# Normalised, transposed and split token halves: made once and kept in DRAM, or made again for the late round

## The chip, the cores and the metric

One core of a Trainium2 chip runs the whole kernel. The metric is the device time of one execution in microseconds (us), the median of several runs. TensorE (PE) does matmuls and transposes and writes PSUM; VectorE (DVE), ScalarE (ACT) and GpSimd (POOL) do elementwise work; SyncE (SP) issues every DMA of this kernel from one queue, in order. A DMA that has to wait for a semaphore holds all DMAs behind it in that queue.

## The reference

Two sequences (1024 tokens, 1024 channels each) go through two layers:

```
(shift, scale, gate) = silu(c) @ W_ada + b_ada
h = RMSNorm(x) * (1 + scale) + shift
P = h @ W_in                          # all inputs of four mixers
x = x + gate * RMSNorm(concat(A, B, C, D) @ W_out)
```

A is latent attention, B RWKV-7, C Mamba-2, D gated DeltaNet, the last three in both directions; each is gated with a slice z of P.

## The kernel before, in words

A unit is a pair (sequence s, layer l); units 0 to 3 are (0,0), (1,0), (0,1), (1,1). A unit has an in-projection (32 tiles of 128 columns of W_in, for each of two halves of 512 tokens), four mixers and an out-projection. The mixers run in two streams: D, then A on the right side of the on-chip memory, C, then B on the left; a mixer takes the place of the one before it on its side. Every tile of P goes to DRAM and is loaded by the mixer that needs it.

The in-projection of the next unit and the out-projection of the unit before run beside the mixers. Their matmuls are one "bulk" stream on line 458 (`paced`), in groups of five, each group released by a tiny memset on POOL (line 462). The in-projection comes in two rounds. The early round gives the tiles of D and the xbc tiles of C for both halves; the late round gives the other 19 tiles, beginning with zc0 and zc1 (the gate of C) and later wa and rkv (for B), cq (for A). The late round begins with the half that the early round ended with, since this half is still there, and then needs the first half again:

```
early = (0, W_D + W_B), (1, W_D + W_B)
late = (1, W_REST), (0, W_REST)
...
run_in(0, (0, W_D), (1, W_D + W_B))
ahead(MIX * EA // 100, 45, lambda: run_in(0, (0, W_B + W_REST), (1, W_REST)))
```

Unit 0 has the second order, with one change of half more. So of 13 makings of a half, five make a half a second time: (0,0) and (0,1) of unit 0 and the half 0 of units 1, 2 and 3, here called (1,0), (2,0), (3,0) by unit and half.

A half is made by `norm_in`, in two groups of 256 tokens: x is loaded (two DMAs of 512 KB), squared and summed on ACT, scaled on DVE by the root (line 289), transposed in 128x128 blocks on TensorE (line 294), and for each block row written twice by ACT (lines 296 and 298: once in full, once rounded to hh); DVE subtracts the two to give hl (line 299). hh and hl together carry h at nearly full precision, each [128, 8, 512]. Each of these two buffers exists once, so a new half can be written only when the last matmul on the old half has read it. An in-projection tile is 8 x 3 matmuls: wh with hh, wh with hl, wl with hh, where wh and wl are the like parts of the weights, made from w by ACT and DVE (lines 327 and 329) just in time.

The order of the instructions on each engine, the DMA queue among them, is laid down at build time by a planner: it runs a model of the engines over the program and takes, of what is ready in the model, what has the best priority. `ahead` and `behind` spread the priorities of the bulk over those of the mixers.

Of the kernel before, what the change touches and what calls it, by code (L numbers as in the profile page):

```python
# [21 lines left out]
D = 1024  # L22
# [86 lines left out]
class Body:  # L109
    def __init__(self, ctx, tc, A, outs, sl=None):  # L110
        self.tc, self.nc, self.A, self.outs = tc, tc.nc, A, outs
        self.n = 0
        self.side = "left"
        self.span = None
        nc = tc.nc
        self.cp = ctx.enter_context(tc.tile_pool(name="cp", bufs=1))
        self.dr = ctx.enter_context(tc.tile_pool(name="dr", bufs=1, space=DRAM))
        self.banks = 3
        self.held = None
        self.token = self.t(self.cp, [1, 1], tag="token")  # L120
        self.gate, self.run = None, 0
        self.ident = self.const(self.cp, "ident")
        self.blk = self.const(self.cp, "blk")
        self.bsel = self.const(self.cp, "bsel")
        self.cc = self.t(self.cp, [128, 4], tag="cc")
        nc.vector.memset(self.cc[:, 0:1], -0.5)
        nc.vector.memset(self.cc[:, 1:2], EPS)
        nc.vector.memset(self.cc[:, 2:3], 0.5)
        nc.vector.memset(self.cc[:, 3:4], 1.0)
        self.mhalf, self.eps, self.phalf, self.one1 = (self.cc[:, i:i + 1] for i in range(4))  # L130

    def open_io(self, ctx):
        """the pools of the projections"""
        self.pj = self.pool(ctx, "pj")
        self.sp = self.pool(ctx, "sp", 2)
        self.pps = self.pool(ctx, "pps", 2, PSUM)
# [20 lines left out]
    def sumsq(self, ps, col, sq, n, rhs, w, start=True, stop=True):  # L157
        """ps[:, col:col+w] = per-token sums over the channels of sq[:, 128 n : 128 n + 128]"""
        for x in range(2):
            self.nc.tensor.matmul(ps[64 * x:64 * x + 64, col:col + w], sq[:, n * 128 + 64 * x:n * 128 + 64 * x + 64], rhs,  # L160
                                  start=start, stop=stop)
# [98 lines left out]

    def stage_in(self, s, L, l, xsrc, Pd, parts=((0, W_ORDER), (1, W_ORDER))):
        """parts: (token half, tiles); the half of the part before is still there"""
        for hf, names in parts:
            if self.held is None or self.held[0] != (Pd, hf):
                self.spread()
                hh = self.t(self.pj, [128, 8, 512], F32R, tag="hh")
                hl = self.t(self.pj, [128, 8, 512], F32R, tag="hl")
                self.norm_in(s, L, xsrc, hf, hh, hl)
                self.held = (Pd, hf), hh, hl
            for name in names:  # L270
                self.spread()
                self.in_tile(l, name, hf, *self.held[1:], Pd)
# [59 lines left out]
    def out_tiles(self, l, ch, hh, hl, kqs, at=lambda kq: kq):  # L332
        """products of 4 token tiles with a quarter of the columns of w_out, over the quarters kqs of its rows"""
        nc, pj = self.nc, self.pj
        pss = [self.t(self.pps, [128, 2, 256], tag="pj") for _ in range(2)]
        for n, kq in enumerate(kqs):
            w = self.t(pj, [128, 2, 256], tag="w", bufs=2)
            self.dma(w, self.A["w_out"][l, ch, kq // 2][:, (kq % 2) * 512:(kq % 2) * 512 + 512].rearrange("p (k c) -> p k c", k=2))
            with self.urgent():
                wh, wl = self.split_w(w, [128, 2, 256])  # L340
            for i in range(4):
                ps = pss[i // 2][:, i % 2]
                c = slice(i * 128, (i + 1) * 128)
                for k in range(2):
                    a, b = hh[:, at(kq) * 2 + k, c], hl[:, at(kq) * 2 + k, c]
                    first, last = n == 0 and k == 0 and i % 2 == 0, n == len(kqs) - 1 and k == 1
                    for m, (u, w2) in enumerate(((a, wh), (a, wl), (b, wh))):
                        self.paced(TO, ps, u, w2[:, k], dict(start=first and m == 0, stop=last and m == 2, skip_group_check=True))
        return pss
# [50 lines left out]
    def stage_out_last(self, s, L, l, xsrc, od, dst, parts, ctx=None):  # L400
        """the last output in parts (token half, quarters of the rows of w_out, whether the sums begin or end),
        while the mixers of the later quarters still run"""
        nc, v, pj, sp = self.nc, self.nc.vector, self.pj, self.sp
# [52 lines left out]
    def paced(self, n, *mm):  # L456
        """a matmul of a bulk stream: groups of n, each issued after the group before has begun"""
        m = self.nc.tensor.matmul(*mm[:3], **mm[3]).ins  # L458
# [9 lines left out]

# [1 line left out]
    def urgent(self):  # L470
# [8 lines left out]
    def behind(self, p0, p1, n, fs):  # L479
        """emit fs with priorities spread over those from p0 to p1"""  # L480
        keep = self.tc.cur_priority
# [33 lines left out]
    def invert(self, pool, r, d, src):  # L515
        """r = inverses of the unit triangular 32 x 32 diagonal blocks of src, transposed"""
        nc = self.nc
# [14 lines left out]
    def merge(self, pool, psp, r, d, src, dst):  # L532
        """dst = inverse of the unit triangular 64 x 64 blocks of src from the inverses r of their diagonal blocks"""
        nc = self.nc
# [32 lines left out]
    def pair_t(self, psp, dst, src, scale=None):  # L567
        """dst[(c parity, t), (c // 2, x, e)] = transposes of 8 chunks of both heads of src, times scale[(c parity, t), c // 2, x]"""
        ps = self.bank(psp)
# [8 lines left out]
    def dma_pair(self, dst, src, swap):  # L578
        """dst[(x or 1 - x, t), c, e] (DRAM) = src[(c parity, t), (c // 2, x, e)]"""
        sv = src.rearrange("p (j x e) -> p j x e", j=4, x=2)  # L580
# [5 lines left out]
    def head_sum(self, ps, sq, n):  # L586
        """ps[half, i] = sums over the channels of the head of the other half"""
        for i in range(n):
# [3 lines left out]
    def heads_back(self, psp, y):  # L592
        """transposes back to channels: y[(1 - x, t), c, pr, e] -> [(pr, e), x, c, t]"""
        ps = self.t(psp, [128, 512], tag="w")
# [4 lines left out]
    def rows2(self, t, r0, q):  # L599
        """rows r0 to r0 + 256 and quarter q of the tokens"""  # L600
        return t[r0:r0 + 256, q * 256:q * 256 + 256].rearrange("(r p) t -> p r t", r=2)
# [43 lines left out]

# [1 line left out]
    def mixer_b(self, L, Pd, l, od):  # L647
# [8 lines left out]
    def rwkv_norm(self, p, psp, L, Pd, q, y, yd, bon, od, free):  # L656
        """normalisation, bonus and gate of a quarter of the tokens"""
        nc, v = self.nc, self.nc.vector
# [292 lines left out]

# [1 line left out]
    def mixer_d(self, L, Pd, l, od):  # L953
# [120 lines left out]
    def gdn_norm(self, p, psp, L, Pd, q, y, yd, fq, od, free):  # L1074
        """normalisation and gate of a quarter of the tokens"""
        nc, v = self.nc, self.nc.vector
# [163 lines left out]

# [1 line left out]
    def mixer_c(self, L, Pd, l, od):  # L1242
# [149 lines left out]

# [1 line left out]
    def mixer_a(self, L, Pd, l, od):  # L1394
# [103 lines left out]
    def attend(self, p, psp, qd, kd, krd, VO, ot):  # L1498
        """softmax of every head; the maxima of a head are found during the head before"""
        nc, v = self.nc, self.nc.vector  # L1500
# [73 lines left out]
    def mixers(self, L, Pd, l, od, which="dcab"):  # L1574
        """the streams right (d, a) and left (b, c)"""
        p = dict.fromkeys(("left", "right"), self.tc.cur_priority)
# [8 lines left out]
    def last_mixers(self, L, Pd, l, od, io):  # L1585
        """three streams: d, c on the right; b; a in the place of the projections"""
        p0 = self.tc.cur_priority
# [15 lines left out]
    def full(self):  # L1603
# [11 lines left out]
        def run_in(u, *parts):  # L1615
            s, l = units[u]
            if u not in P:
                P[u] = self.t(self.dr, [NWT * 128, 1024], tag="P", bufs=2)
            self.stage_in(s, L[l], l, src(s, l), P[u], parts)

# [15 lines left out]
        def ahead(w, n, f):  # L1636
            """emit f with priorities spread over the next w, n steps"""
            p = self.tc.cur_priority
# [4 lines left out]
        def out_last(parts, ctx=None):  # L1643
            s, l = units[3]
            self.stage_out_last(s, L[l], l, src(s, l), o[3], self.outs[s], parts, ctx)

        early = (0, W_D + W_B), (1, W_D + W_B)
        late = (1, W_REST), (0, W_REST)
# [76 lines left out]
```

## Time and profile before

| | |
|---|---|
| median of 3 runs | 4894.8 us (4888.07 to 4915.18) |
| span of the profiled execution | 4894.9 us |
| TensorE busy | 4389.3 us, 90% |
| VectorE busy | 3343.1 us, 68% |
| ScalarE busy | 2178.9 us, 45% |
| mean granted clock of TensorE | 0.878 of full speed |
| DMA | 671.79 MB, 137 GB/s in the mean |

The profiled execution's own time is its span; nothing that was timed lies around it. Busy time of TensorE counts a matmul from its start to a modelled end, so it is more than the time in which it takes columns. Shares are means over the whole span; what a half costs has to be read where it is made.

### The profile page before, as it was taken

How to read it: one execution, taken by the hardware profiler on the slowest of the kernel's cores; microseconds unless marked ns; L12 is line 12 of the kernel's file. 1: busy time of each engine (PE TensorE's matmuls, PEld its weight loads, DVE VectorE, ACT ScalarE, POOL GpSimd, SP SyncE). 2: the span in 40 equal slices, each digit the busy share in tenths (PEclk: the TensorE clock that was granted, in tenths of full speed). 3: DMA queues.
4: the chain of work that ended last, by engine and by line, in shares of the span. 5: the costliest groups of instructions: out<-in, count | busy, mean ns of one | idle time of the engine just before them, and what ended most of it. 6: DMA issues, size and time to landing. Idle time of an engine off the chain costs nothing.

```text
span 4894.9 us, 100724 instructions
## 1 busy us (share of the span) xinstructions
PE 4389.3 (90%) x38644; PEld 3358.2 (69%) x38644; DVE 3343.1 (68%) x6837; ACT 2178.9 (45%) x4734; POOL 397.6 (8%) x2093
## 2 busy tenths in 40 slices
PE   6879798999997988999989898899989989898997
PEld 3667576766776776756767667776767766776686
DVE  2488877566578787566459778657546968856666
ACT  2444363563434534443454453455344354344333
POOL 0101010000101000000011100000011100000001
PEclk8889898998997987989989798798889979878788
DMA  4444264242453546363345353545145535455224
GB/s 144 136 148 138 99 192 132 87 131 99 135 171 126 160 127 192 109 197 110 112 154 162 109 174 117 174 139 147 63 133 165 163 111 158 130 181 156 85 86 137
DMA packets 495063, 671.79 MB, mean 137 GB/s; under 512 B 149752, under 2 KB 265976, under 8 KB 493560
## 3 DMA queue, kind: packets, MB, share of 16 engines
q1 hardware_dynamic: 494584, 665.36, 43.6%
q8 instruction: 306, 5.01, 0.4%
q14 instruction: 173, 1.42, 0.1%
HBM read 486.53 MB, written 178.57 MB: 136 GB/s over the span
## 4 chain that ended last, share of the span: by engine, by line
PE 49%; DVE 13%; DMA 10%; issue 3%; ACT 3%; SPq 1%; POOL 0%; DVEq 0%; POOLq 0%; ACTq 0%
PE pj L458 21%; PE b L824 3%; PE b L1568 2%; PE b L551 2%; DVE iA L522 1%; PE b L558 1%; SPq L144 1%; PE b L1456 1%; PE b L1555 1%; PE pj L243 1%; PE w L863 1%; DVE wl L329 1%; DVE GT L537 1%; PE b L1524 1%; PE y L1220 1%
## 5 line engine op out<-in xcount | busy, mean ns | idle before, releaser
L458 PE MATMUL pj<-hh,wl 128*128 128x512 f32 (+1 forms) x2048 | 848.2, 415 | 32.0 <-DVE wl L329 18.4
L458 PE MATMUL pj<-hh,wh 128*128 128x512 f32 (+1 forms) x2048 | 854.6, 418 | 11.9 <-DVE iT L529 3.2
L458 PE MATMUL pj<-hl,wh 128*128 128x512 f32 (+1 forms) x2048 | 849.7, 415 | 16.9 <-POOL token L462 16.6
L327 ACT CAST wh<-w 128x512 fp32r<-128x512 f32 x640 | 395.1, 618 | 775.4 <-PE pj L458 495.1
L329 DVE TENSOR_TENSOR wl<-w,wh 128x512 fp32r<-128x512 f32 x640 | 446.6, 699 | 245.3 <-ACT wh L327 211.8
L458 PEld LDWEIGHTS pj<-hh,wl 128*128 128x128 f32 (+1 forms) x2048 | 397.5, 194 | 137.5 <-issue 20.7
L458 PEld LDWEIGHTS pj<-hh,wh 128*128 128x128 f32 (+1 forms) x2048 | 397.6, 194 | 115.3 <-issue 19.9
L458 PEld LDWEIGHTS pj<-hl,wh 128*128 128x128 f32 (+1 forms) x2048 | 396.9, 194 | 113.0 <-POOL token L462 22.9
L462 POOL MEMSET token<- 1x1 f32 x1613 | 143.7, 89 | 3317.1 <-PE pj L458 3307.1
L458 PE MATMUL pj<-wh,hl 128*128 128x256 f32 x896 | 266.6, 310 | 0.7 <-DVE hl L363 0.5
L458 PE MATMUL pj<-wh,hh 128*128 128x256 f32 x768 | 238.7, 311 | 6.3 <-ACT hh L362 4.1
L1559 ACT ACTIVATE pT<-b 128x512 f32<-128x512 f32 x256 | 149.8, 596 | 210.6 <-PE b L1557 207.4
L458 PE MATMUL pj<-wl,hh 128*128 128x256 f32 x768 | 234.0, 305 | 0.0
L294 PE MATMUL pj<-c_ident,x 128*128 128x128 f32 x416 | 118.8, 388 | 109.9 <-ACT hh L298 41.0
L1525 DVE TENSOR_REDUCE mx<-b 128x1 f32<-128x512 f32 x256 | 169.7, 686 | 68.5 <-PE b L1524 66.8
L638 DVE SCALAR_TENSOR_TENSOR cva<-cvi,cw,cva 128x1024 f32<-128x1024 f32 x144 | 183.9, 1279 | 47.4 <-ACT cva L634 29.3
L458 PEld LDWEIGHTS pj<-wh,hl 128*128 128x128 f32 x896 | 181.3, 207 | 14.2 <-issue 6.2
L296 ACT ACTIVATE ht<-pj,shc,gsc 128x256 f32<-128x256 f32 x208 | 118.4, 569 | 156.6 <-PE pj L294 84.0
L828 DVE SCALAR_TENSOR_TENSOR G<-b,Dk,mk 128x128 f32<-128x128 f32 x512 | 143.8, 344 | 61.9 <-PE b L824 61.1
L1568 PEld LDWEIGHTS b<-VO,pT 128*64 128x64 f32 x4096 | 150.2, 151 | 42.6 <-issue 29.4
L824 PE MATMUL b<-AR,BK 64*64 64x128 f32 x2048 | 176.7, 299 | 0.0
L1568 PE MATMUL b<-VO,pT 128*64 128x65 f32 x4096 | 168.4, 238 | 4.7 <-ACT pT L1559 4.3
(403 smaller groups left out, 9407.1 us busy)
## 6 DMA issues: line engine op xcount, KB each, us to landing
w<-w_in SPq DMA_DIRECT2D x512, 256.0 KB
P<-st SPq DMA_DIRECT2D x248, 256.0 KB
x<-x SPq DMA_DIRECT2D x76, 512.0 KB
w<-w_out SPq DMA_DIRECT2D x128, 256.0 KB
G<-P SPq DMA_DIRECT2D x112, 256.5 KB
cvi<-P SPq DMA_DIRECT2D x48, 512.0 KB
f<-acr SPq DMA_DIRECT2D x32, 512.0 KB
bkc<-bkd SPq DMA_DIRECT2D x64, 256.0 KB
```

The source lines that it names most:

```text
L294: nc.tensor.transpose(ps[:, i * 128:(i + 1) * 128], xs[i][:, k * 128:(k + 1) * 128], self.ident)
L296: nc.scalar.activation(ht, ps[:, 0:256], AF.Identity, scale=L.gsc[:, k, s:s + 1], bias=L.shc[:, k, s:s + 1])
L327: nc.scalar.copy(wh, w)
L329: nc.vector.tensor_tensor(wl, w, wh.bitcast(F32), SUB)
L458: m = self.nc.tensor.matmul(*mm[:3], **mm[3]).ins
L462: t = self.nc.gpsimd.memset(self.token, 0.0).ins
L638: nc.vector.scalar_tensor_tensor(a, c[:, j:j + 1024], wt(j, i), a, MUL, ADD)
L824: nc.tensor.matmul(ps[self.half(x ^ a), i * 128:i * 128 + 128], BK[self.half(x), pr, c, a], AR[self.half(x), pr, c].rearrange("p a t -> p ...
L828: v.scalar_tensor_tensor(G[:, x, pr, c, :], ps[:, i * 128:i * 128 + 128], Dk[:, c, 2 * x + pr:2 * x + pr + 1], mk, MUL, MUL)
L1525: v.tensor_reduce(mx[:, n, qt:qt + 1], ps, AX.X, ALU.max, negate=True)
L1559: nc.scalar.activation(pT[kt], ps, AF.Exp)
L1568: nc.tensor.matmul(po[64 * x:64 * x + 64, i, :], pT[kt][:, o:o + 64], VO[:, kt, h, :], start=(kt == 0 and i == 0), stop=(kt == 7), skip_gr ...
```

## The change

A half that a later round needs again is stored in DRAM after it is made (two DMAs of 2 MB from hh and hl); when it is needed again, hh and hl are loaded from there (two DMAs of 2 MB), and `norm_in` is not called. The space in DRAM has two places. The set `twice` holds the five pairs (unit, half) from above; the store is made in the part that begins with the tile sm, the first of W_D. All five makings for the second time become loads, five makings for the first time get stores, the other three stay as they are. Everything else in the diff is comments.

```diff
         self.held = None
+        self.spilled = {}
...
-    def stage_in(self, s, L, l, xsrc, Pd, parts=((0, W_ORDER), (1, W_ORDER))):
-        for hf, names in parts:
+    def stage_in(self, s, L, l, xsrc, Pd, parts, again):
+        for n, (hf, names) in enumerate(parts):
             if self.held is None or self.held[0] != (Pd, hf):
                 self.spread()
                 hh = self.t(self.pj, [128, 8, 512], F32R, tag="hh")
                 hl = self.t(self.pj, [128, 8, 512], F32R, tag="hl")
-                self.norm_in(s, L, xsrc, hf, hh, hl)
+                back = self.spilled.get((s, l, hf))
+                if back is None:
+                    self.norm_in(s, L, xsrc, hf, hh, hl)
+                    if again[n]:
+                        self.spilled[s, l, hf] = back = self.t(self.dr, [2, 128, 4096], tag="hd", bufs=2)
+                        for i, h in enumerate((hh, hl)):
+                            self.dma(back[i], h.bitcast(F32).rearrange("p k t -> p (k t)"))
+                else:
+                    for i, h in enumerate((hh, hl)):
+                        self.dma(h.bitcast(F32).rearrange("p k t -> p (k t)"), back[i])
                 self.held = (Pd, hf), hh, hl
...
-            self.stage_in(s, L[l], l, src(s, l), P[u], parts)
+            self.stage_in(s, L[l], l, src(s, l), P[u], parts, [(u, hf) in twice and names[0] == W_D[0] for hf, names in parts])
...
+        twice = {(0, 0), (0, 1), (1, 0), (2, 0), (3, 0)}
```

## Rows read from the trace of the kernel before

**Rows 1.** The page: busy time, share of the span, instructions.
```profile
PE 4389.3 (90%) x38644; PEld 3358.2 (69%) x38644; DVE 3343.1 (68%) x6837; ACT 2178.9 (45%) x4734; POOL 397.6 (8%) x2093
```
**Rows 2.** Five windows: us, busy us by engine (instructions), clock, DMA share, GB/s.
```profile
261.40:299.80 38.40, 20.49 (x173) 14.21 (x173) 23.70 (x38) 22.49 (x43) 4.13 (x7) 0.69 0.48 121
532.40:569.10 36.70, 13.14 (x56) 6.62 (x56) 33.23 (x71) 20.55 (x43) 3.96 (x7) 0.58 0.14 49
1498.40:1565.20 66.80, 41.02 (x545) 34.30 (x544) 61.06 (x100) 29.38 (x63) 11.36 (x13) 0.62 0.33 107
2736.60:2802.90 66.30, 54.58 (x572) 45.34 (x572) 51.66 (x105) 35.64 (x88) 3.24 (x6) 0.58 0.28 86
3916.30:3981.80 65.50, 47.19 (x518) 39.76 (x517) 54.01 (x106) 32.45 (x76) 5.61 (x8) 0.64 0.25 81
sum 273.70, PE 176.41 PEld 140.23 DVE 223.66 ACT 140.50 POOL 28.30; mean PE 35.28 PEld 28.05 DVE 44.73 ACT 28.10 POOL 5.66
```
**Rows 3.** The same five windows, busy time of line 458 alone.
```profile
sum 273.70, PE 2.19 PEld 1.78; mean PE 0.44 PEld 0.36
```
**Rows 4.** Lines 1361 and 1374, units 0 to 3: durations (ns), first and last start.
```profile
L1361 DVE TENSOR_TENSOR y<-y,t x14: 407/424/428, 511.2 to 535.0; 128x256 f32<-128x256 f32 x14
L1374 PE MATMUL b<-c_ident,zz x16: 271/273/474, 585.1 to 609.7; 128*128 128x128 f32 x16
...
L1361 DVE TENSOR_TENSOR y<-y,t x14: 406/420/426, 1610.3 to 1635.5; 128x256 f32<-128x256 f32 x14
L1374 PE MATMUL b<-c_ident,zz x16: 270/272/273, 1641.3 to 1644.7; 128*128 128x128 f32 x16
...
L1361 DVE TENSOR_TENSOR y<-y,t x14: 408/416/426, 2731.5 to 2784.0; 128x256 f32<-128x256 f32 x14
L1374 PE MATMUL b<-c_ident,zz x16: 271/272/329, 2825.7 to 2832.7; 128*128 128x128 f32 x16
...
L1361 DVE TENSOR_TENSOR y<-y,t x14: 406/418/427, 3917.2 to 3965.7; 128x256 f32<-128x256 f32 x14
L1374 PE MATMUL b<-c_ident,zz x16: 270/272/273, 4005.7 to 4013.9; 128*128 128x128 f32 x16
```
**Rows 5.** Mixer C's tile cvi in unit 0: its loads, first and last.
```profile
L144 SPq DMA_DIRECT2D cvi<-P x6: 320/326/424, 315.0 to 362.9; - x6
```
**Rows 6.** The chain that ended last: start us, us, what (a few pieces).
```profile
1375.35 10.33 DMA o<-G
...
2779.54 5.15 DMA x<-x
...
2863.10 2.98 DMA P<-st
2866.10 2.55 DMA G<-P
...
3131.65 11.50 DMA kr<-P
```
**Rows 7.** Groups by form: count, busy us, mean ns, idle before and releaser.
```profile
L294 PE MATMUL pj<-c_ident,x 128*128 128x128 f32 x416 | 118.8, 388 | 109.9 <-ACT hh L298 41.0 <-DVE x L289 40.8 <-DVE ss L286 27.6
...
L299 DVE TENSOR_TENSOR hl<-ht,hh 128x256 fp32r<-128x256 f32 x208 | 88.2, 429 | 61.1 <-ACT hh L298 60.2
...
L289 DVE TENSOR_SCALAR x<-x,rs 128x1024 f32<-128x1024 f32 x52 | 39.6, 763 | 13.9 <-POOL rs L155 13.1
```
**Rows 8.** Waits of the DMA queue: us in total, times, longest.
```profile
SPq L144 <- PE pj L294: 217.8, 27, 31.9
```
**Rows 9.** Two windows in which the transfer engines are saturated (columns as rows 2).
```profile
1920.00:1930.00 10.00, 10.00 (x89) 9.25 (x85) 3.77 (x7) 5.74 (x10) 0.44 (x5) 0.79 0.97 322
...
3130.00:3145.00 15.00, 10.29 (x125) 8.85 (x123) 5.49 (x14) 8.31 (x20) 0.00 (x0) 0.50 1.02 357
```
**Rows 10.** The 15 us after (1,0) and after (3,0) is first made (columns as rows 2).
```profile
851.00:866.00 15.00, 14.12 (x101) 10.18 (x100) 8.71 (x15) 10.51 (x19) 0.62 (x7) 1.00 0.91 232
3446.00:3461.00 15.00, 15.00 (x136) 10.90 (x135) 13.05 (x33) 6.53 (x11) 0.62 (x7) 1.00 0.28 97
```

## The prediction

> **What bounds the kernel now.** I read the busy shares first, then the two streams that share the engines: the projections (the "bulk", line 458) and the mixers. TensorE shows 90% busy [rows 1]; no other engine is near that. That alone would say "take TensorE work away", but where the bulk stands still says more. I looked for the stretches in which a token half is made from x: from the last matmul of the half before to the first steady one on the new half. The five that the change touches, in order (0,0) again, (0,1) again, (1,0), (2,0), (3,0), are the five windows of [rows 2]: 38.4, 36.7, 66.8, 66.3 and 65.5 us, 273.7 us in all. Line 458 is busy for 2.19 us of them [rows 3], so the bulk really stands. TensorE as a whole is busy for 176.41 us of the 273.7 (64%), at a granted clock of 0.58 to 0.69; VectorE for 223.66 us (82%).
>
> Does anybody wait for the bulk there? For that I looked at mixer C, which needs the tiles zc0 and zc1, the first that a late half gives. Its last use of the states (line 1361) and its first use of zc (line 1374) should follow each other directly. In unit 2 the last of the one starts at 2784.0 and the first of the other at 2825.7, in unit 3 it is 3965.7 and 4005.7, in unit 0 535.0 and 585.1; in unit 1 it is 1635.5 and 1641.3 [rows 4]. So C waits some 41, 39, 49 and 5 us (0.4 us of the last addition taken off) for a half that is being made, and B begins when C ends, in C's place. Unit 0 waits a second time: the first convolution tile of C (line 638 and its loads) starts at 315.0, as soon as (0,0) is made again and its xbc tiles are stored [rows 5]. In unit 2 the chain of waits then goes from a store of a projection tile to the load that mixer B does of it [rows 6]. The bulk bounds these places, not the mixers.
>
> **The change, part by part.**
>
> *Removed.* A half is 32 transposes (416 in 13 halves), 16 splits on VectorE, and 4 scalings [rows 7]. Five of 13 halves go: 160 transposes. By mean durations one half is 32 x 388 ns = 12.4 us of TensorE, and 16 x 429 + 4 x 763 ns = 9.9 us of VectorE; five are 62 and 50 us. This is engine time, not yet time of the span, as transposes wait and overlap. Ten MB of x loads go too. A second thing goes: SP waits 217.8 us, 27 times, for line 294 to free an x buffer, with every load of the mixers queued behind [rows 8]; 5 in 13 of that is 84 us of SP's waits, which I count at nothing by itself, since SP mostly waits anyway; the row shows only that the new wait below replaces an old one.
>
> *Added, the load.* Two transfers of 2.10 MB. The trace has none so large. Where the transfer engines are saturated they move 322 and 357 GB/s [rows 9], so 4.19 MB take 11.7 to 13.0 us alone. An x load of 0.52 MB took 5.15 us in the chain [rows 6], of which 1.5 us are data at those rates: some 3 us of fixed time and queue. Other traffic in the gaps averages 90 GB/s, about 40% of it the x loads that go [rows 2]; the remaining 51 leave about 300 GB/s, hence 14 us. I take 14 + 3, rounded up to 18 us from the last matmul on the old half to the first on the new; the ends are 12 (all alone) and 25 us (the other traffic takes the highest share of the five gaps, 0.48, and about half of 340 GB/s is left). Nothing of the new half can start earlier, as the first matmuls need both tiles whole. The gaps shrink by 20, 19, 49, 48 and 47 us, 183 in all.
>
> The load's wait: the buffers hh and hl are single, so SP waits at the head of its queue for the last matmul on the old half. Behind it stand the weight loads of the next tile, zc's loads and mixer D's loads of kvd. The bulk cannot use the weights before the half is there; D is the stream with slack (it comes before A, and by the order of their instructions A ends before B in every unit). I count nothing, and at most the 12 us of one transfer each for D.
>
> *What the shrunk gaps give.* Each is capped by the wait it feeds.
> - Unit 0: both gaps lie on C's way, 20 + 19 = 39 us, less than the 49 that it still waits. But this must last until B of unit 0 ends at about 1375 + 10 us [rows 6], beside A, which does not begin earlier. I keep two thirds: 26.
> - Unit 1: C waits only 5 us. In that window VectorE is busy 61.06 of 66.8 us [rows 2], so half of the 9.9 us that the half no longer takes there may come back: 5 + 5 = 10.
> - Unit 2: min(48, 41) = 41, less 8, since the earlier bulk now competes in a stretch where TensorE was busy for 54.58 of 66.3 us, 10 of them transposes: 33.
> - Unit 3: min(47, 39) = 39, less 8 likewise: 31.
>
> Sum 100 us. Bounds: 65 if the load takes 25 us, half of unit 0's is lost, VectorE gives nothing back and the competition costs 16 instead of 8 (12 + 5 + 25 + 23); 183 if every gap counts whole.
>
> *Added, the stores.* Five times 4.19 MB to DRAM, queued on SP as soon as the half is whole. No saturated stretch of stores is shown; between the load rate and twice the time I take 12.4 us, upper end 25. They are hidden by the weights already split or loaded (three buffers of each part and two of w, each half tile being 12 matmuls). What is late next is the mixers' own loads. After (1,0) is made the engines are already 91% busy, after (3,0) 28% [rows 10]. I take 5 us of each store as seen: 25 us; ends 0 and 5 x 13 = 65.
>
> How far a small transfer stands behind large ones, the trace shows once: in a stretch with a share of 1.02 [rows 9], the load of kr (128 KB) took 11.50 us [rows 6]. The Trainium skill ("DMA: Bandwidth & Descriptors", section "Queues, rings and completion order") says the same as a rule: each transfer engine consumes the descriptors of one issuer's ring in order. By that rule each 4.19 MB would hold everything behind it for its whole length, and the trace agrees with its 11.50 us. What it would make of the time is the second rival.
>
> *Sum.* 4894.9 (span of the profiled execution, equal to the median 4894.8 within 0.1) - 100 + 25 = **4820 us**. The instruction order of every engine is laid down anew by the planner, which I can't work out; it goes into the range.
>
> **The rivals.**
>
> *Everything comes back.* If TensorE is what counts, C's wait is no cap: the 183 us of gap return less some of the stores. For it: 90% busy. Against it: other mixers' work of 128 us of TensorE lies in the gaps and has to be done. 4895 - 183 + 43 (two thirds of the stores' upper end) = 4755, from 4710 to 4780.
>
> *Absorbed.* The bulk comes earlier, but D and A or the start of the next unit's early half, whose making is not removed, set the pace; only the waits of unit 1's kind remain. For it: eight halves are still made. Against: A does not gate B, and C is seen to wait. 4895 - 40 + 25 = 4880, plus or minus 15.
>
> *The queue takes it back (slower).* Ten transfers at 12.4 us on the one queue, each standing before a load of D, B or the weights on the chain: 124 us against 100, giving 4919. It decides once more than eight of the ten are paid whole. For it: the 11.50 us of kr and the share of 0.91 after (1,0). Against: at the five loads the bulk waits already and that time is in the 18 us; shares in the gaps of 0.14 to 0.48 [rows 2].
>
> That the change does nothing is excluded: a half is stored when its part begins with sm and the pair is in the set, which holds for five halves, and each of these is asked for again after another half was held.
>
> **How the numbers follow.** The forecast (4780 to 4860) has 0.50, everything back 0.18, absorbed 0.18, the queue 0.14. Half a per cent, 24 us, is about what a measurement of this kernel can tell from no change. Below 4870: the first two and a fifth of the third, with a little of the forecast lost to a worse plan, 0.70; within: the rest of the third and the near end of the fourth, 0.17; slower 0.13. For 8 in 10 the range reaches down into the second case and up over the third: 4735 to 4905.
>
> **What would show it.** Right: 256 transposes at line 294, five pairs of loads of hh and hl; at the five places the bulk stands about 18 us; lines 1361 and 1374 follow each other within 10 us in units 2 and 3; C of unit 2 ends some 49 us earlier than now (26 + 10 + 33, less four stores of 5), and the weight loads just after each store are at most 5 us late. Wrong: gaps still over 30 us (the load is slow or issued late, SP's wait for line 458 being long), the same wait at line 1374 for another tile, or D's loads of kvd taking 10 us and D ending after B. If C ends earlier by what is predicted and the span does not follow, the fault is in the survival that I took as two thirds or whole.

## The result, and the profile after

The changed kernel takes 4934.55 us in the median (4920.49 to 4956.91, six runs), the kernel before 4891.43 us in the runs beside it (4876.0 to 4915.18, six runs): a ratio of 1.0078, 95% interval 1.0049 to 1.0108. It is slower by 0.8%; I had forecast 4820 us and a gain. The profiled execution spans 4925.4 us, 30.5 more than before.

The page of after, busy time and transfers, answers to [rows 1]:

```profile
PE 4396.8 (89%) x38484; PEld 3357.3 (68%) x38484; DVE 3297.1 (67%) x6717; ACT 2080.9 (42%) x4534; POOL 383.3 (8%) x2073
...
DMA packets 495060, 703.20 MB, mean 143 GB/s; under 512 B 149753, under 2 KB 265977, under 8 KB 491001
```

The 160 transposes are gone (38644 to 38484 instructions on TensorE), VectorE has 46 us less to do, ScalarE 98. TensorE is not less busy: 4396.8 against 4389.3 us.

The group of the transposes in after answers to the first of [rows 7] (lines have moved by 11: 294 is 305, 458 is 469):

```profile
L305 PE MATMUL pj<-c_ident,x 128*128 128x128 f32 x256 | 71.6, 378 | 62.2 <-DVE ss L297 22.2 <-DVE x L300 20.7 <-ACT hh L309 19.1
```

One of each pair of the new transfers, by their tile in DRAM (durations of the issue in ns, first and last issue):

```profile
L145 SPq DMA_DIRECT2D hd<-hh x5: 319/326/330, 88.0 to 3427.3; - x5
L145 SPq DMA_DIRECT2D hh<-hd x5: 378/442/551, 266.4 to 3933.1; - x5
```

And the DMA queue's wait for an x buffer, which answers to [rows 8]:

```profile
SPq L145 <- PE pj L305: 112.1, 16, 25.5
```

Three windows of after, from the last matmul on the old half to the first on the new, at (1,0), (2,0) and (3,0). They answer to the last three of [rows 2], with the same columns:

```profile
1470.40:1485.40 15.00, 8.44 (x32) 5.63 (x32) 15.00 (x36) 8.45 (x13) 0.23 (x3) 0.81 1.01 387
2735.70:2760.90 25.20, 17.36 (x273) 16.74 (x273) 20.57 (x22) 3.22 (x6) 0.00 (x0) 0.57 0.75 262
3932.90:3954.40 21.50, 8.79 (x122) 8.03 (x121) 21.28 (x27) 2.12 (x4) 1.89 (x2) 0.69 0.67 259
```

15.0, 25.2 and 21.5 us stand where 66.8, 66.3 and 65.5 stood. In unit 0 the bulk stops at 266.2 and at 500.5 and runs steadily again from 279.9 and 516.6, which is 13.7 and 16.1 us, with a few matmuls in between. In all five places together TensorE is idle for 6.6 us until one of the loads ends. And mixer C waits less for zc. Lines 1372 and 1385 of after are the lines 1361 and 1374 of [rows 4], units 0 to 3:

```profile
L1372 DVE TENSOR_TENSOR y<-y,t x14: 406/422/427, 504.1 to 520.4; 128x256 f32<-128x256 f32 x14
L1385 PE MATMUL b<-c_ident,zz x16: 271/273/273, 537.2 to 545.8; 128*128 128x128 f32 x16
...
L1372 DVE TENSOR_TENSOR y<-y,t x14: 406/418/426, 1632.9 to 1658.4; 128x256 f32<-128x256 f32 x14
L1385 PE MATMUL b<-c_ident,zz x16: 272/272/273, 1664.1 to 1667.5; 128*128 128x128 f32 x16
...
L1372 DVE TENSOR_TENSOR y<-y,t x14: 403/416/426, 2727.1 to 2774.8; 128x256 f32<-128x256 f32 x14
L1385 PE MATMUL b<-c_ident,zz x16: 272/273/330, 2781.9 to 2790.3; 128*128 128x128 f32 x16
...
L1372 DVE TENSOR_TENSOR y<-y,t x14: 409/418/425, 3933.8 to 3980.2; 128x256 f32<-128x256 f32 x14
L1385 PE MATMUL b<-c_ident,zz x16: 272/273/330, 3987.0 to 3992.1; 128*128 128x128 f32 x16
```

From the start of the last line 1372 to that of the first line 1385 it is some 7 us in units 2 and 3, where it was 41.7 and 40.0; in unit 0 16.8 us remain of 50.1, and unit 1 keeps its 5.7. So the change does in these places what it was forecast to do, and the time is lost elsewhere. To find it I cut the span into C's stages (first to last instruction of mixer C) and B's (from there to B's last instruction), unit by unit; the few us between and around them do not change. First the four stages of C in the kernel before (the columns are those of [rows 2]):

```profile
169.00:635.00 466.00, 400.71 (x3043) 311.80 (x3041) 361.69 (x670) 205.04 (x408) 53.44 (x256) 0.87 0.42 136
1393.00:1662.00 269.00, 240.48 (x1921) 192.46 (x1920) 221.97 (x443) 123.82 (x267) 29.33 (x151) 0.90 0.40 131
2495.00:2851.00 356.00, 328.09 (x2450) 259.75 (x2450) 279.75 (x522) 163.27 (x320) 43.91 (x209) 0.90 0.46 147
3676.00:4035.00 359.00, 324.72 (x2415) 256.68 (x2414) 276.07 (x514) 161.10 (x311) 47.20 (x211) 0.91 0.46 145
sum 1450.00, PE 1293.99 PEld 1020.70 DVE 1139.48 ACT 653.23 POOL 173.88; mean PE 323.50 PEld 255.18 DVE 284.87 ACT 163.31 POOL 43.47
```

The four stages of C in after:

```profile
176.00:563.00 387.00, 351.66 (x2596) 277.52 (x2596) 282.07 (x518) 156.73 (x304) 44.03 (x231) 0.93 0.50 163
1403.00:1688.00 285.00, 264.15 (x1988) 207.79 (x1988) 225.19 (x436) 114.34 (x242) 29.08 (x168) 0.93 0.44 148
2491.00:2811.00 320.00, 294.02 (x2176) 234.37 (x2174) 257.91 (x458) 129.68 (x235) 42.02 (x203) 0.94 0.51 165
3692.00:4010.00 318.00, 290.30 (x2157) 230.84 (x2156) 257.04 (x458) 128.90 (x229) 42.23 (x204) 0.95 0.52 165
sum 1310.00, PE 1200.13 PEld 950.52 DVE 1022.21 ACT 529.65 POOL 157.36; mean PE 300.03 PEld 237.63 DVE 255.55 ACT 132.41 POOL 39.34
```

The four stages of B in the kernel before:

```profile
635.00:1375.00 740.00, 702.97 (x6640) 508.86 (x6640) 486.10 (x1054) 362.23 (x758) 55.48 (x269) 0.94 0.44 130
1662.00:2474.00 812.00, 736.77 (x7054) 546.84 (x7052) 535.97 (x1144) 355.11 (x810) 51.84 (x278) 0.88 0.47 145
2851.00:3644.00 793.00, 724.49 (x7024) 564.00 (x7024) 535.31 (x1133) 360.25 (x823) 51.27 (x300) 0.87 0.44 136
4035.00:4846.00 811.00, 747.25 (x7358) 601.51 (x7359) 545.44 (x1143) 349.31 (x825) 49.33 (x305) 0.84 0.43 131
sum 3156.00, PE 2911.49 PEld 2221.21 DVE 2102.82 ACT 1426.90 POOL 207.91; mean PE 727.87 PEld 555.30 DVE 525.71 ACT 356.72 POOL 51.98
```

The four stages of B in after:

```profile
563.00:1386.00 823.00, 764.58 (x7133) 560.38 (x7133) 553.22 (x1170) 377.96 (x796) 61.86 (x308) 0.90 0.43 131
1688.00:2477.00 789.00, 702.11 (x6850) 517.62 (x6849) 522.92 (x1127) 344.19 (x793) 46.79 (x230) 0.84 0.47 145
2811.00:3656.00 845.00, 759.24 (x7235) 588.33 (x7234) 543.73 (x1162) 368.44 (x859) 51.59 (x300) 0.85 0.43 132
4010.00:4878.00 868.00, 789.27 (x7598) 625.64 (x7595) 556.69 (x1181) 365.83 (x875) 49.36 (x309) 0.83 0.41 125
sum 3325.00, PE 3015.20 PEld 2291.97 DVE 2176.56 ACT 1456.41 POOL 209.59; mean PE 753.80 PEld 572.99 DVE 544.14 ACT 364.10 POOL 52.40
```

C's stages are 140 us shorter, B's 169 us longer; the difference is the 30 us of the span. The counts of TensorE (the first number in parentheses) show what has happened. C's stages hold 912 instructions fewer, of which 160 are the transposes; B's hold 740 more. The same view of the bulk's line alone gives 3293 and 3314 bulk matmuls beside C, 5459 and 5429 beside B. Hence, without bulk and transposes, 773 instructions have left C's stages and 770 have come into B's. Mixers C and B lie whole in their own stages. Counted by line, and for the merging helper by tile, those that moved are mixer D's: it has 3696 matmuls beside C and 2956 beside B in the kernel before, 2919 and 3725 in after, while mixer A lies beside B in both. What ran while C waited now runs beside B. Unit by unit B's stage gains 493, -204, 211 and 240 instructions and 83, -23, 52 and 57 us; in units 0 and 1 that is partly the bulk (165 more and 216 fewer).

### The profile page after: what moved, and what is told of

Read it like the earlier page. It is cut to its first block, busy times and chain, and to the rows that moved or that the text cites. A ratio compares the mean times of both kernels' runs of the same rounds, so it can differ in the third digit from the quotient of the medians.

```text
span 4925.4 us, 99855 instructions
## 1 busy us (share of the span) xinstructions
PE 4396.8 (89%) x38484; PEld 3357.3 (68%) x38484; DVE 3297.1 (67%) x6717; ACT 2080.9 (42%) x4534; POOL 383.3 (8%) x2073
## 5 line engine op out<-in xcount | busy, mean ns | idle before, releaser
L469 PEld LDWEIGHTS pj<-hl,wh 128*128 128x128 f32 (+1 forms) x2048 | 399.5, 195 | 113.3 <-POOL token L473 16.8
L469 PE MATMUL pj<-wh,hl 128*128 128x256 f32 x896 | 280.9, 325 | 20.1 <-DVE hl L374 15.4
L469 PE MATMUL pj<-wl,hh 128*128 128x256 f32 x768 | 244.3, 318 | 0.0
L469 PEld LDWEIGHTS pj<-wh,hl 128*128 128x128 f32 x896 | 193.1, 220 | 36.1 <-DVE hl L374 16.9
L469 PEld LDWEIGHTS pj<-wh,hh 128*128 128x128 f32 x768 | 167.1, 218 | 49.9 <-ACT st L383 19.1
L835 PE MATMUL b<-AR,BK 64*64 64x128 f32 x2048 | 188.2, 310 | 4.5 <-DVE G L839 4.2
L835 PEld LDWEIGHTS b<-AR,BK 64*64 64x64 f32 x2048 | 134.9, 151 | 59.6 <-issue 49.8
L1214 ACT ACTIVATE SE<-SC,el 64x64 f32<-64x64 f32 x480 | 140.2, 338 | 80.4 <-DVE SC L1225 45.3
```

The lines of the kernel that those rows point to most:

```text
L835: nc.tensor.matmul(ps[self.half(x ^ a), i * 128:i * 128 + 128], BK[self.half(x), pr, c, a], AR[self.half(x), pr, c].rearrange("p a t -> p ...
L1214: nc.scalar.activation(SE[half(x), pr], VS[half(x), x, pr, i, :], AF.Identity, scale=el[half(x), d, pr, c:c + 1])
```

## The experiments

**The theories.** M (moved work): the wait of C was not idle time, its work moves into B's stage, and the span is then set by the order in which everything is laid down. Q (the queue): the ten large transfers hold up the loads behind them. R (the order by chance): any disturbance of the planner moves the time by as much, and the change itself pays. In the expectations M is called 'crowding', Q 'transfers' and R 'plan'. Each run is compared with the kernel before on the same chip.

**Each kernel laid down anew.** In e1_stores all five second makings stay, and the five stores are made as well.

```diff
-                if back is None:
+                if True:
                     self.norm_in(s, L, xsrc, hf, hh, hl)
-                    if again[n]:
+                    if back is None and again[n]:
...
-                else:
-                    for i, h in enumerate((hh, hl)):
-                        self.dma(h.bitcast(F32).rearrange("p k t -> p (k t)"), back[i])
```

> The five stores are made, but no half is loaded: each is made again as before (the output is the reference's). Theory 'crowding' (mixer C is finished earlier, but the right stream D, A and then B lose that time again to each other and to the earlier bulk): the stores are hidden, ratio to before 0.997 to 1.004. Theory 'transfers' (the stores hold the mixers' small loads on the one queue): ratio 1.006 to 1.012, that is 5 x 6 to 12 us. Theory 'plan' (any new order of instructions moves the time by this much): anything from 0.992 to 1.010, with no link to the stores.

In e2_one_store only the first half is stored and every load reads that one; in e3_free there is neither store nor load, and the late round works on whatever the tiles hold. The edit of e3_free against the changed kernel (the lines that ask for hh and hl also move into the first branch):

```diff
...
-                        self.spilled[s, l, hf] = back = self.t(self.dr, [2, 128, 4096], tag="hd", bufs=2)
-                        for i, h in enumerate((hh, hl)):
-                            self.dma(back[i], h.bitcast(F32).rearrange("p k t -> p (k t)"))
+                        self.spilled[s, l, hf] = True
...
                 else:
-                    for i, h in enumerate((hh, hl)):
-                        self.dma(h.bitcast(F32).rearrange("p k t -> p (k t)"), back[i])
+                    hh, hl = self.held[1:]
```

> Only the first half is stored, and all five loads read it (four of the five loads bring the wrong half). Crowding: as the changed kernel, 1.004 to 1.011, with D and A as late. Transfers: 0.990 to 1.000, since four of five stores are gone. Plan: anything between.

> No store and no load: in the five places the tiles that are there are used again (the wrong half), so that a half made anew costs nothing at all and the bulk never stands there. It is the bound of what the change could give. Crowding: 0.99 to 1.01; mixer C ends 40 to 70 us earlier in units 0, 2 and 3 and B gives it back. Transfers: 0.965 to 0.985, as the 100 us of the forecast come whole. Plan: the mean effect of the removed work, 0.98, with a scatter of 0.01.

The fourth is the kernel before with nothing changed but the number by which the bulk's priorities are spread, 1800 in both kernels:

```diff
-MIX = 1800
+MIX = 1790
```

> The kernel before with MIX 1790 in place of 1800, which shifts the priorities of the late rounds by half a per cent: no work is changed, only the planner's order. Crowding and transfers: 0.998 to 1.002. Plan: off by 0.003 to 0.010 one way or the other.

Measured: e1_stores 1.0151 (1.012 to 1.0181), e2_one_store 0.9973 (0.9943 to 1.0002), e3_free 0.9834 (0.9802 to 0.9866), e4_replan 1.0272 (1.0236 to 1.0308). Taken alone, the first three look like a plain answer for Q: stores cost 1.5%, and without any transfer the change gains 1.7%. (For M e3_free is a miss: 0.99 to 1.01 was expected.) The fourth forbids the plain answer. A half per cent in one parameter, with the same work and the same transfers, costs 2.7%, more than any of the three shows and more than R itself had expected. Differences between kernels that are laid down anew say little of the part that was edited.

**The order of the kernel before, held.** So the order was taken out. Each engine's instructions that both kernels have got an order-only edge to the one before them on the engine, as the plan of the kernel before had it. Such an edge puts no semaphore into the program; only the added instructions are placed anew.

```diff
...
+            for e, names in engines.items():
+                last = None
+                for n in names:
+                    i = common.get(n)
+                    if i is None:
+                        continue
...
+                    if last is not None:
+                        tc.add_manual_dep(i, last.name, NOSYNC, reason="plan")
+                    last = i
...
```

> The whole change, but every instruction that both kernels have keeps, on each engine, the order of the kernel before (order-only edges, no semaphore); only the five second makings are missing, and five pairs of stores and loads are put in between. Theory 'plan' (the loss of the change comes from the planner's new order, not from the stores, the loads or the shorter gaps): ratio to before 0.980 to 0.993, faster by some of the 75 us of the forecast. Theory 'crowding' (what C gains, B gives back to D and A on the shared engines): 0.997 to 1.006, as with the new order. Theory 'transfers': 1.003 to 1.010.

> As p1_change_old_order, without the stores and the loads: in the five places the tiles that are there are used again (the wrong half). Plan: 0.975 to 0.990, faster than p1 by 0 to 0.006. Crowding: 0.995 to 1.003. Transfers: 0.975 to 0.985 with p1 at least 0.012 above it.

> The five stores alone in the order of the kernel before, every half is made again as before. e1_stores (planned anew) lay at 1.015. Plan: 1.000 to 1.005, so that two thirds or more of e1's loss was its order. Transfers: 1.008 to 1.016, as e1. Crowding: 1.000 to 1.003.

Measured: the change in the old order 1.0025 (0.9991 to 1.0059), the same with both transfers free 0.9971 (0.9937 to 1.0004), the stores alone 1.0036 (0.9999 to 1.0073). In the old order no loss and no gain is clear of the noise. R had expected a gain of 0.7% or more in the first two and is wrong there, Q misses all three, and M's ranges hold the first two. Why nothing is gained is seen in two windows of p2_free_old_order, those where units 2 and 3 change to the late half:

```profile
2714.60:2777.80 63.20, 46.44 (x541) 40.97 (x540) 42.91 (x82) 16.19 (x48) 0.41 (x2) 0.57 0.28 88
3894.20:3956.50 62.30, 43.40 (x485) 38.46 (x484) 45.13 (x83) 12.54 (x36) 2.29 (x4) 0.53 0.26 83
```

The half needs no making and no loading, and still the bulk stands for 63 and 62 us. In the old order 540 and 484 instructions of the mixers stand on TensorE between the last bulk matmul on the old half and the next one: those that stand there in the kernel before, without the 32 transposes. The gap belongs to the order, not to the making alone.

**The order of the changed kernel, held.** The same edges with the changed kernel's order: q1_no_stores and q2_free as e2 and e3 above, and q3_nosp with the five makings put back in place of stores and loads (its DMA queue alone is laid down anew).

> The changed kernel with every instruction that is kept held in the changed kernel's own order; only the first half is stored and all five loads read that one, so four stores are gone and units after the first store project a wrong half. Changed kernel 1.0078 of the one before. Theory P (the stores are paid, 0.3 to 0.4% as measured in the old order): 1.004 to 1.005. Theory Q (the stores hold up the one DMA queue, and that is the whole slowdown): 0.995 or less. Theory O (only the order counts): 1.007 to 1.009.

> The same order held, with no store and no load: the late round reads whatever the two tiles hold, so its products are of another half. It is the changed kernel with both transfers free. Theory P: stores 0.35% and loads of five times some 15 us 0.5 to 1.5%: 0.990 to 0.999. Theory O (only the order counts): 1.005 to 1.008. In both, the sum of B's stages stays at 3260 to 3330 us, if it is the order that stretches them; it falls to 3200 or less, if the transfers do.

> The five second makings put back (no store, no load), with the common instructions of TensorE, VectorE, ScalarE and GpSimd held in the changed kernel's order; only the DMA queue is laid down anew. If the changed kernel's order is a poor one and the change itself is worth the 1.0% of the mean over four orders: 1.015 to 1.03, slower than the changed kernel by 0.7 to 2%. If the change is worth nothing at any order and only moves the gaps: 1.00 to 1.01, as the changed kernel. If remaking is better at any order, as the three orders with a slower time would not have shown: below 1.00.

Measured: q1_no_stores 1.0067 (1.0039 to 1.0095), q2_free 1.0048 (1.0026 to 1.0069), q3_nosp 1.0249 (1.0209 to 1.0288). Q falls with the first. Its interval takes in P and O; that of the second, where nothing is transferred, reaches into O and not down to P. The third says that the change is worth something in this order. The new order, too, has its own gaps of the bulk. In q2_free, without any load, it stands at (1,0), (2,0) and (3,0) for

```profile
1463.40:1476.60 13.20, 8.06 (x32) 5.65 (x33) 13.20 (x32) 7.34 (x11) 0.23 (x3) 0.84 0.42 147
2727.90:2752.80 24.90, 17.32 (x272) 16.70 (x273) 20.60 (x22) 3.19 (x6) 0.00 (x0) 0.58 0.29 96
3926.40:3948.60 22.20, 10.48 (x120) 9.60 (x120) 21.06 (x27) 2.02 (x4) 1.89 (x2) 0.58 0.18 60
```

that is, for nearly the 15.0, 25.2 and 21.5 us of the changed kernel. Stages of C, then of B, of q3_nosp, units 0 to 3:

```profile
174.00:595.00 421.00, 370.07 (x2659) 287.50 (x2658) 300.57 (x565) 194.41 (x384) 48.94 (x239) 0.88 0.44 139
1430.00:1735.00 305.00, 272.33 (x2018) 211.94 (x2018) 233.97 (x459) 133.05 (x282) 31.39 (x172) 0.90 0.40 128
2540.00:2884.00 344.00, 305.75 (x2218) 240.53 (x2217) 268.52 (x483) 149.72 (x275) 44.49 (x207) 0.90 0.47 147
3769.00:4112.00 343.00, 303.18 (x2185) 237.84 (x2184) 266.06 (x481) 147.94 (x268) 45.27 (x208) 0.91 0.47 147
...
595.00:1414.00 819.00, 760.33 (x7133) 558.96 (x7133) 553.27 (x1170) 377.66 (x796) 61.93 (x308) 0.91 0.43 127
1735.00:2526.00 791.00, 711.28 (x6849) 528.97 (x6850) 521.99 (x1127) 343.03 (x793) 46.29 (x229) 0.84 0.47 140
2884.00:3733.00 849.00, 767.10 (x7221) 593.50 (x7220) 543.90 (x1162) 367.66 (x857) 51.10 (x300) 0.83 0.42 126
4112.00:4978.00 866.00, 788.92 (x7597) 629.69 (x7595) 557.01 (x1182) 365.42 (x877) 50.27 (x309) 0.84 0.42 126
```

The six cells side by side. Stage sums and TensorE counts are from the same view of each kernel, one profiled execution each (that of p2_free_old_order is the fastest of its twelve):

| order | late half | time to before | C, us | C, PE instr. | B, us | B, PE instr. |
|---|---|---|---|---|---|---|
| old | made (before) | 1 | 1450 | 9829 | 3156 | 28076 |
| old | loaded (p1) | 1.0025 | 1449 | 9668 | 3190 | 28071 |
| old | free (p2) | 0.9971 | 1429 | 9676 | 3141 | 28069 |
| new | made (q3) | 1.0249 | 1413 | 9080 | 3325 | 28800 |
| new | loaded (after) | 1.0078 | 1310 | 8917 | 3325 | 28816 |
| new | free (q2) | 1.0048 | 1302 | 8902 | 3329 | 28820 |

B's stages take 3325 to 3329 us in the new order, whether the half is made, loaded or free, and 3141 to 3190 in the old. So it is the order, with some 740 instructions more beside B, that lengthens B; the transfers do not (Q falls). The transfers cost 1.0078 - 1.0048 = 0.3% in the new order, some 15 us, and 0.54%, some 26 us, in the old. By the intervals these are uncertain by 0.4 and 0.5%, so they are hardly clear of nothing and at most some 1%. The stores alone are 0.36% in the old order; without four of the five the new one gains 0.1%, inside the interval. And the change is worth 1.7% in its own order (1.0249 to 1.0078), while in the old one its 0.25% of loss lies inside the interval: the new order suits the changed kernel, the old one gives it nothing.

**Orders chosen for neither.** What is left is whether the change pays under an order that was picked for neither kernel. Both kernels were run with the spreading number at five values; the edit is the line of e4_replan.

> The changed kernel with MIX 1790, to be set against e4_replan, the kernel before with MIX 1790, at 1.027 of the kernel before. Plan: its ratio to the kernel before may be anything from 0.985 to 1.03, and its ratio to e4 need not have the sign of that at MIX 1800. Crowding and transfers: 1.004 to 1.011 above e4, so 1.031 to 1.038.

> The kernel before with MIX 1780: another order, the same work. MIX 1790 (e4_replan) lay at 1.027 of the kernel before. If the order is worth per cents by itself, and 1800 is a good order among its neighbours: 1.005 to 1.03. If 1790 was an outlier: 0.997 to 1.005.

> The kernel before with MIX 1820, as b1780: 1.005 to 1.03 if the order is worth per cents and 1800 is a good one, 0.997 to 1.005 if 1790 was an outlier.

> The changed kernel with MIX 1780 (at 1800 1.0078 and at 1790, with almost the same order, 1.0054 of the kernel before). If the change is worth nothing in the mean over orders: within 0.01 of b1780. If its work saved counts: 0.985 to 0.995 of b1780 in the mean of the pairs. In every order without second makings, C's stages summed over the units lie at 1300 to 1320 us and B's at 3250 to 3340, against 1440 to 1490 and 3150 to 3250 with them: so crowding.

> The changed kernel with MIX 1820, to be set against b1820 as a1780 against b1780: within 0.01 of it if the change is worth nothing in the mean over orders, 0.985 to 0.995 if the work saved counts; C's stages shorter and B's longer by about as much in either case.

> The kernel before with MIX = 1840. So far the setting moves the kernel before by 0 to 2.7% (mean 1.0116 over 1780, 1790, 1800, 1820), 1800 being its best. If the order is a matter of luck: 1.00 to 1.03.

> The changed kernel with MIX = 1840. If the change is worth about 1% under an order that is not chosen for either kernel: 0.3 to 2% below the kernel before with MIX = 1840. If it is worth nothing: the same as that one, or slower.

| MIX | before | changed | changed / before |
|---|---|---|---|
| 1780 | 1.0127 (1.0087 to 1.0168) | 0.9993 (0.9962 to 1.0024) | 0.987 |
| 1790 | 1.0272 (1.0236 to 1.0308) | 1.0054 (1.0022 to 1.0087) | 0.979 |
| 1800 | 1 | 1.0078 (1.0049 to 1.0108) | 1.008 |
| 1820 | 1.0066 (1.004 to 1.0092) | 0.9952 (0.9917 to 0.9987) | 0.989 |
| 1840 | 1.022 (1.0177 to 1.0264) | 1.0118 (1.0074 to 1.0161) | 0.990 |

1800 is the best of the five for the kernel before and the only one at which the change loses; at the other four it gains 1.0 to 2.1%. The mean over five is -1.0%, with a scatter of 1.1% from setting to setting, which five settings do not tell from nothing; over the four others it is -1.4%, with a scatter of 0.5%. The changed kernel at 1820 (0.9952, 0.9917 to 0.9987) is the fastest version that leaves nothing out, and it beats both kernels; it is the best of five draws, so a little of that is selection.

Where does the time go at the other settings? The stages, cut as above, one profiled execution each:

| MIX | C before, us | C changed, us | B before, us | B changed, us | change of C and B together, us |
|---|---|---|---|---|---|
| 1780 | 1486 | 1309 | 3172 | 3311 | -38 |
| 1790 | 1487 | 1312 | 3246 | 3334 | -87 |
| 1800 | 1450 | 1310 | 3156 | 3325 | +29 |
| 1820 | 1474 | 1330 | 3192 | 3279 | -57 |
| 1840 | 1464 | 1348 | 3246 | 3312 | -50 |

At every setting C's stages become shorter and B's longer, so M names the place (with the change C at 1820 and 1840 lies 10 and 28 us above the 1300 to 1320 that were expected, all the other sums lie in their ranges). But B gives back all of it at 1800 alone; elsewhere 38 to 87 us of C's 116 to 177 are kept. M as it was put for e5_after_1790, with the same loss at any order (1.031 to 1.038), is refuted by 1.0054. Nor does the number of instructions beside B set its length by itself: of the five settings of the kernel before, 1800 has the most (28076, the others 27757 to 28019) and the shortest B. So R holds for the sign of the result, M for the place where the time went.

## Why the prediction was wrong, by its steps

**Removed: right.** 256 transposes at line 305, and the queue's wait for x falls by 106 us, from 217.8 to 112.1, where 84 was reckoned (and counted at nothing).

**The load: the size right, by luck.** 18 us were forecast for each gap, bounds 12 to 25; 13.7, 16.1, 15.0, 25.2 and 21.5 were measured. But the forecast made the gap out of the transfer's length, and q2_free has nearly the last three gaps without any transfer (13.2, 24.9, 22.2). There the mixers' instructions that the order puts in front of the next bulk matmul fill the gap (272 and 120 in units 2 and 3), and in after TensorE is idle for the loads for 6.6 us in all.

**C's wait: right in place, too small in unit 0.** I forecast 26, 10, 33 and 31 us; C's stages became shorter by 79, -16, 36 and 41, 140 in sum where the bulk's term was 100. C of unit 2 ends 40 us earlier (49 were forecast). In unit 0 the wait at zc itself shrinks by 33 us (50.1 to 16.8); the other 46 of the 79 lie earlier in the stage, which also holds 447 instructions of TensorE fewer. Unit 1 gives nothing: its stage holds 67 instructions more than before, with 99 bulk matmuls more in it.

**The survival: the step that failed.** "Each is capped by the wait it feeds" took C's wait as time that leaves the span, with two thirds kept in unit 0 and the whole, less 8 us, in units 2 and 3. None of it was kept at the setting that was asked about. The number that should have stopped me was in [rows 2]: TensorE was busy for 176 of the 274 us of the gaps, mostly with other mixers' work. I used it against the rival "everything comes back" ("has to be done") and not against my own term: work that is done while C waits has to be done later too, and it is done beside B, on an engine that is 90% busy. The counts show it go there (773 out, 770 in), and the six cells show that B's 169 us more come with the order that has it there, and not with the transfers. How much is kept depends on the order: at the other four settings it is 38 to 87 us. TensorE was idle for 97 us of the gaps (273.7 - 176.4); that this is the bound on what can be kept is an estimate, which these four do not contradict and which no run tests by itself.

**The order: left in the range, and too small there.** "The instruction order of every engine is laid down anew by the planner, which I can't work out; it goes into the range" was true, but the range had room for 85 us above the forecast, and an edit of half a per cent in one parameter moves this kernel by 2.7%, 130 us. The profile could not show that. Only the runs at other settings did, and with them that the time before is the best of five draws.

**The stores: right within their interval.** 25 us were forecast; 0.36% in the old order is 18 us (0 to 36).

**The rivals.** "The queue takes it back" gives 4919, the nearest number, by the wrong cause (it is the third in the list; the prediction once calls it the second). In the new order without any transfer 1.0048 remains, and all ten transfers cost 15 to 26 us (at most some 50 by the intervals), where that rival had 124. The rule behind it is that of the Trainium skill ("DMA: Bandwidth & Descriptors", section "Queues, rings and completion order"): each transfer engine consumes the descriptors of an issuer's ring in order. No run here tests the rule itself: shares of 0.67 to 1.01 stand in the three windows of the loads, which shows the engines full and not in what order small transfers landed. What the runs show is that a transfer's length is not its price here. "Absorbed" came nearest in mechanism, in that the pace is not set by C's wait, but it kept a gain of 15 us, and D and A as the pace were not tested by a run.

**What stays open.** Why the two orders differ by 0.8% for the very same work (q2_free and p2_free_old_order) is read only, below, and no experiment isolates it. Nor does one say why B gives back more than C gains at 1800 and half to four fifths elsewhere.

## What to carry to other kernels

Take a wait of one stream as a gain at most as far as the busy engine is idle in it: before you subtract it, count the other streams' instructions in it and say in which later stage they will run, and whether that stage is on the chain. Where a planner lays down the order, an edit is two changes, the work and the order: hold the order to price the work, and run both kernels over a few settings to judge the edit, since a setting that happens to be the best for one kernel favours that one.

## What the runs showed of the chip beyond that

**The two orders differ in the granted clock more than in idle time.** The cores' view of q2_free, then of p2_free_old_order, which do the same work:

```profile
core 0: 4919.6 us, clock 0.873
```

```profile
core 0: 4858.0 us, clock 0.883
```

Over the runs of each the mean clock is 0.872 and 0.877, of the changed kernel 0.871, of the kernel before 0.877 to 0.879 in the runs beside the experiments. In the two profiles TensorE is busy for 4408.9 and 4331.2 us with the same 38484 instructions, so that 511 and 527 us are idle: the slower order is not the one with more idle time. (The second profile is the fastest execution of its kernel; the medians differ by 42 us, the profiles by 62.) The five settings of the kernel before, the same work in five orders, point the same way: the mean clock of their runs is 0.877 to 0.879, 0.876, 0.874, 0.866 and 0.861 where the time is 1, 1.0066, 1.0127, 1.022 and 1.0272. It is not the whole of it, as the changed kernel has 0.871 both at 1800 (1.0078) and at 1820 (0.9952). In after, C's stages run at 0.93 to 0.95, up from 0.87 to 0.91, and B's at 0.83 to 0.90, down from 0.84 to 0.94 (rows above). A stretch of B in unit 2, the inverses and their merging, in before and in after:

```profile
3014.00:3112.00 98.00, 84.90 (x932) 76.16 (x933) 79.59 (x181) 45.03 (x130) 8.94 (x50) 0.90 0.40 127
```

```profile
2960.00:3086.00 126.00, 103.06 (x1051) 94.62 (x1052) 95.43 (x177) 36.09 (x103) 7.94 (x50) 0.72 0.31 95
```

It takes 28 us longer, with the clock at its lower level (1.2 of 2.4 GHz) for more of the time: 0.72 in the mean instead of 0.90. 368 of the 932 matmuls there are the bulk's in before, 351 of 1051 in after. The two stretches hold the same inverse of B but not the same work beside it: in after 256 matmuls of the merging of D's inverse lie in it too, which in before are done by 2977, ahead of the stretch. So the 28 us are not the clock's alone. That the order costs its time by way of the clock is read from these rows; no edit has changed the one without the other.
